# Layer 1 FFN up products: GpSimd's sums behind the gating, VectorE's block sums ahead of it and two blocks later

## The chip, the cores and the metric

The kernel runs on one core of one Trainium2 chip. The metric is the device time of one execution in microseconds; a kernel's time is the median over several executions. The engines are named as the profile names them: PE (TensorE matmul), PEld (its weight load), DVE (VectorE), ACT (ScalarE), POOL (GpSimd) and SP (the queue that issues the DMAs).

## What is computed

A two-layer trunk over 1024 latent and 256 context tokens, width 1024. Layer 0 mixes tokens by pooling, layer 1 by attention. Each layer ends with a gated FFN with a three-tap convolution over positions:

```
u = h @ w_up                       # (1024, 1024) @ (1024, 5632)
u = up[:-2]*conv_w[0] + up[1:-1]*conv_w[1] + up[2:]*conv_w[2] + conv_b
a, v = split(u, 2);  y = (silu(a) * v) @ w_down      # (1024, 2816) @ (2816, 1024)
```

The change lies in layer 1's `h @ w_up` and in what is prepared beside it for `@ w_down`.

## The kernel before

**Three matmuls for one.** Every float32 operand is split into a high part (a rounding copy on ACT, line 160) and a low part (source minus high part, line 161, mostly on POOL, some on DVE). `mm3` (lines 164 to 166) multiplies high by high, high by low and low by high.

**Blocks.** The 2816 gate columns and the 2816 value columns are cut into 22 blocks of 128. Block j works on gate columns and value columns j together, over 1024 tokens. Two columns of blocks and two halves of the inner dimension form a 2x2 by 2x2 block product, which is done with seven products instead of eight (Winograd's form of Strassen's scheme). In block j >= 3 PE runs products 1, 6, 2, 5, 7, 3, 4 in that order; each is 4 times `mm3`, 12 matmuls of 128x512. Products 6 and 5 share PSUM bank 6, products 7 and 4 share bank 4, products 1 and 2 share bank 0 or 2, by the block's parity. Block 0 is a plain product and blocks 1 and 2 mix in with it; they have their own order of products (`order`).

**What surrounds the products.** For block j the seven products need sums of the weights (`w_sums`, four on POOL, line 1492, from the raw weights `wraw` to the buffers `sf`) and six splits (`w_split`: 5 is the raw gate block, 1024 columns wide, 1, 0, 2, 3 are the sums, 4 the lower half of the raw value block; 512 wide). After the products come, from `up_acts`:

- a copy of product 1's bank by ACT (`s1c`, line 1567), which product 2 has to wait for;
- five DVE additions that read or write PSUM (`plus`, line 1528): `vsum` after product 6 (product 5 waits for it), `rsum` after 5, b3 after 7 (product 4 waits for it, since it adds to the bank that b3 reads), b1 after 3, b2 after 4;
- for either half: `ident` on ACT (line 1539, PSUM to SBUF with scale and bias), then two taps on DVE (line 1547); Silu on ACT for the gate half (line 1554);
- `gating` on DVE (line 1556, 128x1024, both inputs in SBUF), and the store of its result to `g_d[j]` in DRAM.

**Sums for the down projection.** The product with `w_down` is also done in seven products, of 11 blocks each, and needs sums of weights (`weights_sums`, stored to `tw_d`) and of gated units (`units_sums`, stored to `sg_d`): four 128x512 DVE operations per set (line 1673), both inputs in SBUF. From block 3 on, each block carries one set: sets of weights 0 to 7 in blocks 3 to 10, sets of units 0 to 10 in blocks 11 to 21; three sets of weights are done at the start of the down products. The buffers are `sum_a` and `sum_b`; loads and stores go through SP.

**The order on each engine.** A function that is due at time t in `acts` is issued as soon as the planned matmuls before it add up to t (`play`); a `mm3` of 512 columns is planned at 0.648 us, a product at 2.592, a block at 18.144. `end[j, p]` is the planned end of product p of block j. So due times set the order of instructions on each engine, and each engine runs its own in that order. For block j of the steady part, counted from the planned start of the block, DVE has before the change: vsum at 5.18, gating of block j-1 at 5.28, that block's four sums for the down projection at 6.63 to 9.93, rsum at 10.37, b3 at 12.96, b1 at 15.60, two taps, b2 at 18.45, two taps. POOL has the four `w_sums` of block j+1 from 0.30 on and its six low parts from 4.40 to 7.40.

Of the kernel before, what the change touches and what calls it, by code (L numbers as in the profile page):

```python
# [10 lines left out]
F32 = mybir.dt.float32  # L11
# [71 lines left out]
def backbone(ctx: ExitStack, tc: tile.TileContext, io, out: bass.AP):  # L83
# [1367 lines left out]
    sf_early, sf_late = ([at(o, HK, P) for o in q] for q in ((172, 174, 144, 146), (128, 130, 108, 110)))  # L1451
    gate_w = [hl(16, KT, P), hl(152, KT, P)]

    gate_early = [tuple(at(o, KT, P, r=True) for o in q) for q in ((108, 128), (136, 168))]
# [16 lines left out]
            nc.sync.dma_start(wraw[j, part], w_up1[:, :, c : c + P])  # L1471

    def sf_of(j):
        return sf_early if j == 1 else sf_late

    gate_third = at(136, KT, P, r=True), at(104, KT, P, r=True)
    sum_third = [hl(o, HK, P) for o in (96, 100, 16, 20, 196)]
# [19 lines left out]
    def w_split(j, which):
# [32 lines left out]
    def up_acts(j, end):  # L1530

        b = banks_of(j)
        b0, b1, bx, b2, b3 = (bank(n) for n in (b[1], b[3], 6, 4, 5))
        cv = conv[1]

        def ident(half):
            f = half * NJ + j
            src = psum[:, b[1] * 512 : (b[1] + 2) * 512] if half == 0 else psum[:, 4 * 512 : 6 * 512]
            nc.scalar.activation(cs1[half], src, AF.Identity, scale=cv[:, 1, f : f + 1], bias=cv[:, 3, f : f + 1])  # L1539

        def tap(half, t):
# [47 lines left out]
    def t_lo(m, eng):  # L1589
        eng.tensor_tensor(out=tsp[m][1], in0=tfs[m], in1=tsp[m][0].bitcast(F32), op=ALU.subtract)  # L1590
# [48 lines left out]
    acts += [(18.5, lambda: t_lo(1, nc.vector)), (18.6, lambda: t_lo(0, nc.vector))]  # L1639
    acts += [(18.7, lambda: w_split(1, 3)), (18.8, lambda: w_split(1, 0)), (18.9, lambda: w_load(2)), (20, lambda: w_split(1, 4)), (20.1, lambda: w_split(2, 5))]  # L1640
    acts += [(19 + 0.1 * n, lambda m=m, q=q: t_hi(m, q)) for n, (m, q) in enumerate(((2, 0), (2, 1), (3, 0), (3, 1)))]
    acts += [(end[0, "gate"] + 3, lambda: t_lo(2, nc.vector)), (end[0, "value"] + 3, lambda: t_lo(3, nc.vector))]
    for j in range(NJ):
        acts += up_acts(j, end)
    for j in range(2, NJ):
        t = end[j - 2, 4]
        for q in range(4):
            acts.append((t + (5.05 + 0.6 * (q - 2) if j == 2 and q > 1 else 0.3 + 0.01 * q), lambda j=j, q=q: w_sums(j)[q]()))
        for q, which in enumerate((5, 1, 0, 2, 3, 4)):
            if j > 2 or q:  # L1650
                acts.append((t + 4.4 + 0.6 * q, lambda j=j, which=which: w_split(j, which)))
        if j + 1 < NJ:
            acts.append((t + 0.1, lambda j=j: w_load(j + 1)))

# [17 lines left out]
    def tt2(o, x, y, op):  # L1672
        return lambda: nc.vector.tensor_tensor(out=o, in0=x, in1=y, op=op)  # L1673
# [4 lines left out]
    def units_sums(f):

        a11, a21 = sum_a[:, 0], sum_a[:, 1]  # L1680
        a12, a22 = cs1[1][:, 0:HC], cs1[1][:, HC:LAT]
        s1, s4 = sum_b[:, 0], sum_b[:, 1]

        def keep_sums():
            nc.sync.dma_start(sg_d[f][0], sum_a.rearrange("p a b -> p (a b)"))
            nc.sync.dma_start(sg_d[f][1], sum_b.rearrange("p a b -> p (a b)"))

        return [tt2(s1, a21, a22, ALU.add), tt2(a21, a11, a21, ALU.subtract), tt2(a11, s1, a11, ALU.subtract),
                tt2(s4, a12, a11, ALU.subtract), keep_sums]
# [12 lines left out]

    def sums_acts(j):

        t21 = max(end[j, 4] + 0.05, max(end[j, 3], end[j, 5] + 0.75) + 2.9)
        t = max(t21 + 4.1, end.get((j + 1, 6), 0) + 0.1)
        if j < NH2:
            f = j - 3
            r = [(end[j, 4] + 0.2, lambda: sums_load(w_dn[f], sum_a)), (end[j, 4] + 0.21, lambda: sums_load(w_dn[f + NH2], sum_b))]
            fns = weights_sums(f, sum_a, sum_b)  # L1710
        else:
            f = j - NH2
            r = [(end[j, 4] + 0.2, lambda: sums_load(g_d[f], sum_a))]
            fns = units_sums(f)
        return r + [(t + 1.35 + 1.1 * n, fn) for n, fn in enumerate(fns)]
# [140 lines left out]
```

## Time and profile before

| | us |
|---|---|
| median of 3 runs (lowest, highest) | 2270.13 (2269.89, 2270.99) |
| the profiled execution, its own time | 2274.05 |
| span of the profiled execution, first to last instruction | 2272.3 |
| PE busy in it | 2176.8 (96%) |
| DVE, POOL, ACT busy | 1466.7, 1368.6, 982.8 |

The profile is one execution. Busy shares are averages over stages that have different limits; matmuls are pipelined, so the start-to-start distance of matmuls tells more of PE's pace than their busy time.

### The profile page before, as it was taken

The numbers are of one execution on the slowest core, as the hardware profiler recorded it, in microseconds if no ns is written. First come the engines' busy times: TensorE is split into PE (matmuls) and PEld (weight loads), VectorE is DVE, ScalarE is ACT, GpSimd is POOL, SyncE is SP. The second block draws the span as 40 slices with busy tenths as digits, with TensorE's granted clock in tenths as the row PEclk, the third lists the DMA queues.
The fourth block names the chain that finished last, engine by engine and source line by source line (L and its number), as shares of the span: only waits on it lengthen the run. The fifth ranks groups of instructions, "written<-read, shape, count | busy, mean of one in ns | idle before, by whom it ended". The sixth has DMA issues, their size and how long they took to land.

```text
span 2272.3 us, 29713 instructions
## 1 busy us (share of the span) xinstructions
PE 2176.8 (96%) x11008; PEld 1794.8 (79%) x11008; DVE 1466.7 (65%) x1986; ACT 982.8 (43%) x1519; POOL 1368.6 (60%) x846
## 2 busy tenths in 40 slices
PE   7989999999999999999999999999999999999999
PEld 5768888888888878877877887777777777778887
DVE  5665545544556484457776666655768888888565
ACT  4364333433434233444446666644433333334442
POOL 0344666666665556753346777634677787764655
PEclk8999999999999999999999999999999999999999
DMA  8831221122127667740000122132235544448775
GB/s 312 290 124 58 68 83 61 61 82 70 61 77 245 214 239 237 242 154 19 32 21 24 62 65 75 47 102 78 81 102 177 194 162 144 158 157 327 258 241 184
DMA packets 191891, 306.06 MB, mean 135 GB/s; under 512 B 12658, under 2 KB 120066, under 8 KB 191746
## 3 DMA queue, kind: packets, MB, share of 16 engines
q1 hardware_dynamic: 191746, 304.17, 40.1%
q8 instruction: 86, 1.41, 0.3%
q14 instruction: 59, 0.48, 0.1%
HBM read 237.26 MB, written 66.86 MB: 134 GB/s over the span
## 4 chain that ended last, share of the span: by engine, by line
PE 59%; DVE 23%; ACT 6%; issue 6%; DMA 3%; POOL 2%; SPq 0%; ACTq 0%; DVEq 0%; POOLq 0%
PE psum L164 18%; PE psum L166 18%; PE psum L165 18%; DVE a L1673 5%; PE psum L1292 2%; DVE a L1547 2%; DVE a L1556 2%; ACT a L1539 2%; DVE a_512r L161 1%; DVE psum L1528 1%; DVE a L1274 1%; DVE a L1127 1%; POOL a_1024r L161 1%; DVE a L1035 1%; ACT a_512r L160 1%
## 5 line engine op out<-in xcount | busy, mean ns | idle before, releaser
L161 POOL TENSOR_TENSOR a_512r<-a,a_512r 128x512 fp32r<-128x512 f32 x366 | 539.3, 1491 | 297.0 <-ACT a_512r L160 265.9
L160 ACT CAST a_512r<-a 128x512 fp32r<-128x512 f32 (+1 forms) x509 | 291.6, 610 | 476.9 <-POOL a L621 188.0
L161 POOL TENSOR_TENSOR a_1024r<-a,a_1024r 128x1024 fp32r<-128x1024 f32 x106 | 273.3, 2581 | 260.3 <-ACT a_1024r L160 247.3
L164 PE MATMUL psum<-a_2048r,a_512r 128*128 128x512 f32 (+1 forms) x1008 | 358.7, 356 | 25.2 <-DVE psum L1528 20.3
L166 PE MATMUL psum<-a_2048r,a_512r 128*128 128x512 f32 (+1 forms) x1008 | 355.2, 353 | 0.0
L165 PE MATMUL psum<-a_4096r,a_512r 128*128 128x512 f32 x708 | 278.1, 393 | 0.0
L683 DVE SCALAR_TENSOR_TENSOR a<-psum,conv,a 128x255 f32<-128x255 f32 (+1 forms) x176 | 150.8, 879 | 147.6 <-ACT a L678 146.0
L164 PEld LDWEIGHTS psum<-a_2048r,a_512r 128*128 128x128 f32 x1008 | 191.4, 190 | 61.3 <-DVE psum L1528 27.4
L165 PE MATMUL psum<-a_2048r,a_512r 128*128 128x256 f32 (+1 forms) x688 | 231.2, 336 | 0.0
L161 DVE TENSOR_TENSOR a_512r<-a,a_512r 128x512 fp32r<-128x512 f32 (+1 forms) x143 | 141.8, 997 | 134.1 <-ACT a_512r L160 129.5
L166 PEld LDWEIGHTS psum<-a_2048r,a_512r 128*128 128x128 f32 x1008 | 191.0, 189 | 26.3
L164 PE MATMUL psum<-a_1024r,a_512r 128*128 128x512 f32 x440 | 172.5, 392 | 1.9 <-ACT a L1093 1.1
L166 PE MATMUL psum<-a_1024r,a_512r 128*128 128x512 f32 x440 | 171.4, 390 | 1.0 <-DVE a_512r L161 1.0
L165 PE MATMUL psum<-a_1024r,a_512r 128*128 128x512 f32 x440 | 171.3, 389 | 0.0
L1539 ACT ACTIVATE a<-psum,conv 128x1024 f32<-128x1024 f32 x44 | 53.1, 1206 | 264.5 <-DVE psum L1528 264.5
L164 PE MATMUL psum<-a_4096r,a_1024r 128*128 128x512 f32 x408 | 161.5, 396 | 2.7 <-ACT a L1567 2.7
L166 PE MATMUL psum<-a_4096r,a_1024r 128*128 128x512 f32 x408 | 159.9, 392 | 1.8 <-POOL a_1024r L161 1.8
L165 PE MATMUL psum<-a_4096r,a_1024r 128*128 128x512 f32 x408 | 159.4, 391 | 0.0
L164 PE MATMUL psum<-a_4096r,a_512r 128*128 128x512 f32 x388 | 152.9, 394 | 1.8 <-ACT a L716 1.8
L165 PEld LDWEIGHTS psum<-a_4096r,a_512r 128*128 128x128 f32 x708 | 133.8, 189 | 25.7 <-POOL a_4096r L767 0.4
L166 PE MATMUL psum<-a_4096r,a_512r 128*128 128x512 f32 x388 | 152.4, 393 | 0.0
L1547 DVE SCALAR_TENSOR_TENSOR a<-psum,conv,a 128x1023 f32<-128x1023 f32 x88 | 112.9, 1282 | 60.2 <-ACT a L1539 58.7
(241 smaller groups left out, 5001.2 us busy)
## 6 DMA issues: line engine op xcount, KB each, us to landing
a<-in_ada_w_dram SPq DMA_DIRECT2D x96, 512.0 KB
a<-in_ffn_w_up_dram SPq DMA_DIRECT2D x88, 512.0 KB
a<-in_ffn_w_down_dram SPq DMA_DIRECT2D x88, 512.0 KB
g_d<-a SPq DMA_DIRECT2D x44, 512.0 KB
x_d<-a SPq DMA_DIRECT2D x26, 512.0 KB
tw_d<-a SPq DMA_DIRECT2D x22, 512.0 KB
sg_d<-a SPq DMA_DIRECT2D x22, 512.0 KB
a<-tw_d SPq DMA_DIRECT2D x44, 256.0 KB
```

Of the source, the lines that this page charges most:

```text
L160: nc.scalar.copy(hi, src)
L161: (lo_eng or nc.gpsimd).tensor_tensor(out=lo, in0=src, in1=hi.bitcast(F32), op=ALU.subtract)
L164: nc.tensor.matmul(ps, lh, rh, start=first, stop=False, skip_group_check=shared)
L165: nc.tensor.matmul(ps, lh, rl, start=False, stop=False, skip_group_check=shared)
L166: nc.tensor.matmul(ps, ll, rh, start=False, stop=last, skip_group_check=shared)
L683: nc.vector.scalar_tensor_tensor(out=dst[:, lo:hi], in0=src[:, lo + d : hi + d], scalar=cv[:, t, f : f + 1], in1=dst[:, lo:hi], op0=ALU.mu ...
L1035: nc.vector.tensor_scalar(out=o, in0=pt[:, q * P : (q + 1) * P], scalar1=sc, scalar2=sh, op0=ALU.mult, op1=ALU.add)
L1292: nc.tensor.transpose(pt[:, h * P : (h + 1) * P], probs[(4 * u + h) % len(probs)][:, k * P : (k + 1) * P], ident)
L1539: nc.scalar.activation(cs1[half], src, AF.Identity, scale=cv[:, 1, f : f + 1], bias=cv[:, 3, f : f + 1])
L1547: nc.vector.scalar_tensor_tensor(out=c[:, lo:hi], in0=psum[:, o + lo + d : o + hi + d], scalar=cv[:, t, f : f + 1], in1=c[:, lo:hi], op0=A ...
L1556: (tg, lambda: nc.vector.tensor_tensor(out=cs1[1], in0=cs1[0], in1=cs1[1], op=ALU.mult)),
L1673: return lambda: nc.vector.tensor_tensor(out=o, in0=x, in1=y, op=op)
```

## The change

For blocks 4 to 21 the weight sums on POOL are due only after the gating of the block before (planned 0.3 us after product 6's end, 0.2 after the gating's due time), and their first buffer is moved to offset 188, where the gating's first input (`cs1[0]`) lies, so they also have to wait for it. The low parts are spread over the block: the raw gate block's split and the raw value block's split around the block's start, splits 0 and 1 between the sums, splits 2 and 3 after product 1 of the next block. The Silu is due after product 1 of the next block. On DVE the four sums for the down projection are due right behind vsum, ahead of the gating, and block j's own set is done in block j instead of behind the gating of block j in block j+1: sets of weights 0 to 9 in blocks 3 to 12, sets of units 0 to 8 in blocks 13 to 21 (two blocks later than before); weights 10 and units 9 and 10 are done at the start of the down products. The units' sums are made from two loads instead of one load and the gating's result in SBUF; the loads are due in product 7 of the block before. The halves of the second stored sum change places, so products 3 and 5 of the down projection read each other's half. Product 1 of block 2 comes ahead of product 7 of block 1, product 6 of block 2 ahead of its product 2, and the convolution of block 0 and two low parts (`t_lo(2)`, `t_lo(3)`) are due at other times.

```diff
-    sf_early, sf_late = ([...] for q in ((172, 174, 144, 146), (128, 130, 108, 110)))
+    sf_early, sf_late, sf_gate = ([at(o, HK, P) for o in q] for q in ((172, 174, 144, 146), (128, 130, 108, 110), (188, 130, 108, 110)))
...
-        return sf_early if j == 1 else sf_late
+        return sf_early if j == 1 else sf_late if j < 4 else sf_gate
...
-                (t12 + 3.8, lambda: nc.scalar.activation(cs1[0], cs1[0], AF.Silu)),
+                (max(t12 + 3.8, end.get((j + 1, 1), 0) + 0.15 if j else 0), lambda: nc.scalar.activation(cs1[0], cs1[0], AF.Silu)),
...
-            t12, t21 = end[0, "gate"] - 0.75, end[0, "value"] + 0.95
-            return conv_of(t12, t21, t21 + 4.1)
-        t12 = max(end[j, 3], end[j, 5] + 0.75) + 0.05
+            fns, t = [fn for _, fn in conv_of(0, 0, 0)], end[0, "value"]
+            times = end[0, "gate"] + 0.05, t - 4.5, t - 3.5, t + 0.3, t + 0.05, end[1, 6] + 0.02, end[1, 6] + 0.03, end[1, 6] + 0.3, end[1, 6] + 1.6
+            return list(zip(times, fns))
+        t12 = max(end[j, 3], end[j, 5] + 0.75, end[j, 7]) + 0.05
...
-    order = [(1, 6), (1, 3), (1, 5), (1, 7), (2, 1), (1, 4)] + [(2, p) for p in (2, 6, 5, 7, 3, 4)]
+    order = [(1, 6), (1, 3), (1, 5), (2, 1), (1, 7), (1, 4)] + [(2, p) for p in (6, 2, 5, 7, 3, 4)]
...
-    acts += [(end[0, "gate"] + 3, lambda: t_lo(2, nc.vector)), (end[0, "value"] + 3, lambda: t_lo(3, nc.vector))]
+    acts += [(end[1, 6] + 0.1, lambda: t_lo(2, nc.vector)), (end[1, 6] + 0.2, lambda: t_lo(3, nc.vector))]
...
+        else:
+            hi, lo = ([lambda j=j, w=w, h=h: split_parts(j, w)[h]() for w in range(6)] for h in range(2))
+            sums = [lambda j=j, q=q: w_sums(j)[q]() for q in range(4)]
+            tg, tn = end[j - 1, 6] + 0.3, end[j, 1]
+            acts += [(t - 1.4, hi[5]), (t - 0.5, lo[5]), (t + 0.06, hi[4]), (t + 0.07, lo[4]),
+                     (tg, sums[0]), (tg + 1.3, hi[0]), (tg + 1.31, sums[1]), (tg + 2.6, hi[1]), (tg + 2.61, lo[0]),
+                     (tg + 3.9, lo[1]), (tg + 5.2, sums[2]), (tg + 6.5, sums[3]),
+                     (tn + 0.05, hi[2]), (tn + 0.06, hi[3]), (tn + 0.07, lo[2]), (tn + 0.08, lo[3])]
...
+    side_sums = [(w_dn, weights_sums, f) for f in range(NH2 - 1)] + [(g_d, units_sums, f) for f in range(NH2)]
+    side_sums.append((w_dn, weights_sums, NH2 - 1))
     for j in range(3, NJ):
-        acts += sums_acts(j)
+        src, make, f = side_sums[j - 3]
+        fns, stores = make(f, sum_a, sum_b)
+        t = end[j, 6] + 0.02
+        acts += [(end[j - 1, 7] + 0.1 + 0.01 * q, lambda src=src, f=f, q=q, w=w: sums_load(src[f + q * NH2], w))
+                 for q, w in enumerate((sum_a, sum_b))]
+        acts += [(t + 0.01 * m, fn) for m, fn in enumerate(fns)] + [(t + 3 + 0.1 * q, fn) for q, fn in enumerate(stores)]
...
+    for n, m in enumerate((2, 0, 1)):
+        src, make, f = side_sums[NJ - 3 + m]
...
+        t = (base - 4.5, base - 4.4, base + 10)[n]
...
+        t = base + (8.2, 13.8, 20.2)[n]
+        acts += [(t + 1.36 * q, fn) for q, fn in enumerate(fns)] + [(t + 5.5 + 0.1 * q, fn) for q, fn in enumerate(stores)]
```

## Rows read from the trace of the kernel before

**Rows 1.** Waits from 1690 to 2040 us: which instruction's line waited for which, us in total, times, longest.
```profile
PEld psum L164 <- DVE psum L1528: 27.4, 17, 2.0
PE psum L164 <- DVE psum L1528: 20.3, 17, 1.5
```

**Rows 2.** Timeline of PE: the first matmuls of blocks 3, 4 and 21 and of the down products, and around the wait ahead of product 4 in blocks 4 and 20 (the first and the last of 17). Columns: start, duration, engine, line, operation, tiles, shapes, idle before and who ended it.
```profile
1669.38 0.39 PE L164 MATMUL psum<-a_4096r,a_1024r 128*128 128x512 f32 x1
...
1688.63 0.39 PE L164 MATMUL psum<-a_4096r,a_1024r 128*128 128x512 f32 x1
...
1706.78 0.50 PE L164 MATMUL psum<-a_2048r,a_512r 128*128 128x512 f32 x1 [1.54 <-DVE psum L1528]
...
2033.47 0.39 PE L166 MATMUL psum<-a_4096r,a_512r 128*128 128x512 f32 x1
2035.03 0.50 PE L164 MATMUL psum<-a_2048r,a_512r 128*128 128x512 f32 x1 [1.18 <-DVE psum L1528]
...
2037.88 0.39 PE L164 MATMUL psum<-a_4096r,a_1024r 128*128 128x512 f32 x1
...
2056.92 0.39 PE L164 MATMUL psum<-a_512r 128*128 128x512 f32 x1
```

**Rows 3.** Timeline of DVE over one block of the steady part, the same columns.
```profile
1777.22 0.68 DVE L1528 TENSOR_TENSOR a<-psum,a 128x512 f32<-128x512 f32 x1
1777.82 2.79 DVE L1556 TENSOR_TENSOR a<-a,a 128x1024 f32<-128x1024 f32 x1
1780.53 1.77 DVE L1673 TENSOR_TENSOR a<-a 128x512 f32<-128x512 f32 x1
1782.34 3.36 DVE L1673 TENSOR_TENSOR a<-a,a 128x512 f32<-128x512 f32 x2
...
1787.33 0.68 DVE L1528 TENSOR_TENSOR a<-psum,a 128x512 f32<-128x512 f32 x1
1788.11 1.30 DVE L1528 TENSOR_TENSOR psum<-psum,a 128x512 f32<-128x512 f32 x2
1790.74 2.60 DVE L1547 SCALAR_TENSOR_TENSOR a<-psum,conv,a 128x1023 f32<-128x1023 f32 x2 [1.33 <-ACT a L1539]
1793.26 0.69 DVE L1528 TENSOR_TENSOR psum<-psum,a 128x512 f32<-128x512 f32 x1
1795.22 2.60 DVE L1547 SCALAR_TENSOR_TENSOR a<-psum,conv,a 128x1023 f32<-128x1023 f32 x2 [1.27 <-ACT a L1539]
```

**Rows 4.** Timeline of POOL over the same stretch.
```profile
1777.12 2.41 POOL L161 TENSOR_TENSOR a_1024r<-a,a_1024r 128x1024 fp32r<-128x1024 f32 x1 [3.97 <-ACT a_1024r L160]
1779.49 9.04 POOL L161 TENSOR_TENSOR a_512r<-a,a_512r 128x512 fp32r<-128x512 f32 x5
...
1789.84 3.79 POOL L1492 TENSOR_TENSOR a<-a,a 128x512 f32<-128x512 f32 x3
```

**Rows 5.** Block 3, which carries no sums for the down projection, and block 21, where POOL has almost nothing to do: DVE's timeline (b1 of block 3, two sums of block 21) and POOL's (one row each).
```profile
1686.12 0.70 DVE L1528 TENSOR_TENSOR psum<-psum,a 128x512 f32<-128x512 f32 x1 [2.02 <-PE psum L166]
...
2048.01 0.69 DVE L1673 TENSOR_TENSOR a<-a 128x512 f32<-128x512 f32 x1
2048.74 0.69 DVE L1673 TENSOR_TENSOR a<-a,a 128x512 f32<-128x512 f32 x1
...
1678.20 7.25 POOL L161 TENSOR_TENSOR a_512r<-a,a_512r 128x512 fp32r<-128x512 f32 x5
2043.89 3.53 POOL L161 TENSOR_TENSOR a_512r<-a,a_512r 128x512 fp32r<-128x512 f32 x2 [9.20 <-ACT a_512r L160]
```

**Rows 6.** The chain of work that ended last, within 1777 to 1800 us, in order of time: start, us, what.
```profile
1787.43 3.35 DMA tw_d<-a
1790.79 7.44 DMA a<-in_ffn_w_down_dram
```

**Rows 7.** Timeline of PE between blocks 1 and 3: the last matmul ahead of the first of four gaps, the matmuls behind the other three, and one of those that follow the third.
```profile
1632.11 0.39 PE L166 MATMUL psum<-a_4096r,a_512r 128*128 128x512 f32 x1
...
1639.09 0.47 PE L164 MATMUL psum<-a_2048r,a_512r 128*128 128x512 f32 x1 [2.41 <-DVE a L1547]
1650.19 0.50 PE L164 MATMUL psum<-a_4096r,a_1024r 128*128 128x512 f32 x1 [2.67 <-ACT a L1567]
1652.22 0.63 PE L165 MATMUL psum<-a_4096r,a_1024r 128*128 128x512 f32 x1
1658.36 0.50 PE L164 MATMUL psum<-a_2048r,a_512r 128*128 128x512 f32 x1 [0.79 <-DVE a L1528]
```

**Rows 8.** The same stretch on DVE, POOL and ACT: the taps of block 0 and `t_lo(2)`, the first weight sum of block 2, and the copy `s1c` of block 2.
```profile
1628.11 2.60 DVE L1547 SCALAR_TENSOR_TENSOR a<-psum,conv,a 128x1023 f32<-128x1023 f32 x2 [2.09 <-ACT a L1539]
1630.63 2.32 DVE L1590 TENSOR_TENSOR a_2048r<-a,a_2048r 128x2048 fp32r<-128x2048 f32 x1
...
1631.19 2.89 POOL L1492 TENSOR_TENSOR a<-a 128x512 f32<-128x512 f32 x1 [0.40 <-DMA a<-in_ffn_w_up_dram]
1649.57 0.57 ACT L1567 COPY a<-psum 128x512 f32<-128x512 f32 x1
```

**Rows 9.** Granted clock (the column behind the engines' busy times), DMA share and GB/s over two stretches, and PE's one wait over half a microsecond in the down products.
```profile
1690.00:2040.00 350.00, 329.73 (x1433) 267.31 (x1432) 300.55 (x240) 125.48 (x170) 275.31 (x167) 1.00 0.49 161
1630.00:1660.00 30.00, 22.94 (x91) 17.55 (x90) 20.71 (x17) 13.62 (x18) 28.71 (x19) 0.94 0.42 124
...
2090.67 0.50 PE L166 MATMUL psum<-a_512r 128*128 128x512 f32 x1 [0.50 <-DVE a_512r L161]
```

More of the change, by code (lines that the diff above doesn't have):

```diff
@@ L1450, in backbone @@
     raws = Ring(at(o, D) for o in (168, 172, 208, 212))
-    sf_early, sf_late = ([at(o, HK, P) for o in q] for q in ((172, 174, 144, 146), (128, 130, 108, 110)))
+    sf_early, sf_late, sf_gate = ([at(o, HK, P) for o in q] for q in ((172, 174, 144, 146), (128, 130, 108, 110), (188, 130, 108, 110)))
     gate_w = [hl(16, KT, P), hl(152, KT, P)]
@@ L1495, in w_sums, with split_parts @@
                 op(3, a12, sf[1], ALU.subtract)]
+    def split_parts(j, which):
+        (hi, lo), src = (gate_of(j), wraw[j, 0]) if which == 5 else (
+            sums_of(j)[which], sf_of(j)[which] if which < 4 else wraw[j, 1][:, HK:])
+        return (lambda: nc.scalar.copy(hi, src),
+                lambda: nc.gpsimd.tensor_tensor(out=lo, in0=src, in1=hi.bitcast(F32), op=ALU.subtract))
     def w_split(j, which):
@@ L1646, in backbone @@
         t = end[j - 2, 4]
[L1647 to L1653, printed above, removed]
+        acts += [(t + 0.1, lambda j=j: w_load(j + 1))] if j + 1 < NJ else []
+        if j < 4:
+            for q in range(4):
+                acts.append((t + (5.05 + 0.6 * (q - 2) if j == 2 and q > 1 else 0.3 + 0.01 * q), lambda j=j, q=q: w_sums(j)[q]()))
+            for q, which in enumerate((5, 1, 0, 2, 3, 4)):
+                if j > 2 or q:
+                    acts.append((t + 4.4 + 0.6 * q, lambda j=j, which=which: w_split(j, which)))
+        else:
[6 more added lines that the diff above has]
+                     (tn + 0.05, hi[2]), (tn + 0.06, hi[3]), (tn + 0.07, lo[2]), (tn + 0.08, lo[3])]
     NH2, HC = NJ // 2, 512
@@ L1665, in backbone @@
     G_AT = {1: lambda f: g_d[f][:, 0:HC], 2: lambda f: g_d[f + NH2][:, 0:HC], 4: lambda f: g_d[f + NH2][:, HC:LAT],
-            5: lambda f: sg_d[f][1][:, 0:HC], 3: lambda f: sg_d[f][1][:, HC:LAT],
+            3: lambda f: sg_d[f][1][:, 0:HC], 5: lambda f: sg_d[f][1][:, HC:LAT],
             6: lambda f: sg_d[f][0][:, 0:HC], 7: lambda f: sg_d[f][0][:, HC:LAT]}
@@ L1676, in sums_load, with kept @@
         nc.sync.dma_start(dst.rearrange("p a b -> p (a b)"), src)
[L1678 to L1689, printed above, removed]
+    def kept(dst, wa, wb):
+        return [lambda q=q, w=w: nc.sync.dma_start(dst[q], w.rearrange("p a b -> p (a b)")) for q, w in enumerate((wa, wb))]
@@ L1691, in weights_sums, with units_sums @@
+    def units_sums(f, wa, wb):
+        a11, a21, a12, a22 = wa[:, 0], wa[:, 1], wb[:, 0], wb[:, 1]
+        return [tt2(a22, a21, a22, ALU.add), tt2(a21, a11, a21, ALU.subtract), tt2(a11, a22, a11, ALU.subtract),
+                tt2(a12, a12, a11, ALU.subtract)], kept(sg_d[f], wa, wb)
     def weights_sums(f, wa, wb):
         b11, b12, b21, b22 = wa[:, 0], wa[:, 1], wb[:, 0], wb[:, 1]
-        def keep_sums():
-            nc.sync.dma_start(tw_d[f][0], wa.rearrange("p a b -> p (a b)"))
-            nc.sync.dma_start(tw_d[f][1], wb.rearrange("p a b -> p (a b)"))
@@ L1698, in weights_sums @@
         return [tt2(b11, b12, b11, ALU.subtract), tt2(b12, b22, b12, ALU.subtract), tt2(b22, b22, b11, ALU.subtract),
-                tt2(b21, b21, b22, ALU.subtract), keep_sums]
+                tt2(b21, b21, b22, ALU.subtract)], kept(tw_d[f], wa, wb)
     base = span(pe)
[L1703 to L1715, printed above, removed]
@@ L1717, in backbone @@
-    for j in range(3, NJ):
-        acts += sums_acts(j)
-    for n, f in enumerate(range(NH2 - 3, NH2)):
-        wab = [at(o, 2, HC) for o in ((64, 68), (72, 76), (80, 84))[n]]
-        t = (base - 4.5, base - 4.4, base + 0.5)[n]
-        acts += [(t + 0.01 * q, lambda f=f, q=q, w=wab[q]: sums_load(w_dn[f + q * NH2], w)) for q in range(2)]
-        acts += [(base + 13.2 + 1.36 * (4 * n + m), fn) for m, fn in enumerate(weights_sums(f, *wab))]
+    side_sums = [(w_dn, weights_sums, f) for f in range(NH2 - 1)] + [(g_d, units_sums, f) for f in range(NH2)]
@@ new lines, in backbone @@
+    side_sums.append((w_dn, weights_sums, NH2 - 1))
+    for j in range(3, NJ):
+        src, make, f = side_sums[j - 3]
[6 more added lines that the diff above has]
+        src, make, f = side_sums[NJ - 3 + m]
+        wab = [at(o, 2, HC) for o in ((64, 68), (72, 76), (80, 84))[n]]
+        t = (base - 4.5, base - 4.4, base + 10)[n]
+        acts += [(t + 0.01 * q, lambda src=src, f=f, q=q, w=wab[q]: sums_load(src[f + q * NH2], w)) for q in range(2)]
+        fns, stores = make(f, *wab)
+        t = base + (8.2, 13.8, 20.2)[n]
+        acts += [(t + 1.36 * q, fn) for q, fn in enumerate(fns)] + [(t + 5.5 + 0.1 * q, fn) for q, fn in enumerate(stores)]
```

## The prediction

> **What bounds the kernel now.** I read the waits of the stage first. Between 1690 and 2040 us PE waits for one kind of instruction only, an addition of `plus` on DVE, once in each of 17 blocks [rows 1]. PE's timeline shows where: ahead of product 4, which adds to the bank that b3 still has to read. The wait is 1.54 us in block 4 and 1.18 in block 20, where the next matmul starts 1.56 us after the last one instead of 0.23 [rows 2]. Next the block's length. Block 21 has no such wait and takes 2056.92 - 2037.88 = 19.04 us for 84 matmuls; so a product is 2.72 us. Blocks 4 to 20 take (2037.88 - 1688.63) / 17 = 20.54 us, 1.50 more each. Block 3 takes 19.25 [rows 2].
>
> Then DVE's timeline, to see why b3 is late. Gating and the four sums for the down projection stand between vsum and rsum and take from 1777.82 to 1787.4 us, 9.6 us [rows 3]. A sum of 512 elements takes 1.67 to 1.77 us there. In block 21, after POOL's last instruction there, the same operation takes 0.69 [rows 5]. POOL's timeline gives the cause: its low parts run from 1777.12 to 1788.5, five of them at 9.04 / 5 = 1.81 us each; the weight sums that meet only additions and taps, which take one operand from PSUM, need 3.79 / 3 = 1.26 [rows 4]. The taps keep 2.60 the pair meanwhile [rows 3]. So operations with two SBUF inputs on DVE and POOL take turns: 0.6 + 1.26 is the 1.8 of either. Block 3 separates the two: POOL works there, the four sums are absent, and PE has no wait of that kind.
>
> A rule agrees and says who gives way. The Trainium skill, "SBUF — State Buffer", section "Who interferes with whom", states that DVE with two SBUF inputs and a reading GpSimd instruction use one interface, held for a whole instruction by whichever started first. By the rule and by the rows a collision costs the same; what hangs on the rule is only the first rival's mechanism.
>
> **The change, block by block.** I walk one block from 4 on, u = us after its first matmul; products end at 2.72, 5.44, 8.16, 10.88, 13.60, 16.32, 19.04.
>
> DVE: b1 starts 0.2 after product 3 (block 3: 1686.12, against 1688.63 - 2.72 = 1685.91 [rows 2, 5]), at u = 16.5. From b1's start (1788.76) to the end of the last tap (1797.82) DVE and ACT need 9.06 [rows 3], so the taps end at 25.6, 6.55 of the next block. vsum follows until 7.2. Now come the four sums, while POOL should be idle: 4 x 0.7 = 2.8 [rows 5], until 10.0. The gating is never seen alone; from below it is two 512-wide operations at 0.6, 1.2; from above it is today's 2.79 [rows 3]. I take 1.2, since POOL waits for it: 11.2. With 0.5 for a meeting with POOL's last low part (below) it ends at 11.7. rsum ends at 12.4, b3 (product 7 + 0.2 + 0.7) at 14.5, and product 4 starts at 16.32 without waiting: 1.8 to spare.
>
> POOL: sum 0 starts at 11.7. Two sums and low part 0 at 1.27 (low parts lie between 1.26 and block 3's 7.25 / 5 = 1.45, where the gating still interrupts one [rows 4, 5]) end at 15.5; low part 1 and sums 2, 3 at 19.4; the 1024-wide low part (2.41 [rows 4]) at 21.8; low part 4 at 23.1, 4.1 of the next block. Low parts 2 and 3 need ACT: ident starts 1.27 ahead of its taps [rows 3], at 2.7, takes 1.2, then the copy for product 2 (0.57 [rows 8]) ends at 4.5, ahead of that product's start at 5.44, and two casts of 0.6 follow. So these parts run from 5.1 to 7.7 and meet the first DVE sum, which is due at 7.2: the 0.5 above. POOL works 14 us of 19.04. Every operand is ready: product 6 of the next block has low part 1 by 16.8, product 7 has low part 2 by 6.4 against 10.88.
>
> New waits: sum 0 lies in the gating's input buffer. Behind it on POOL wait all the other sums and the splits; ident of the block (u = 17.2) overwrites that buffer and has to wait for low part 0, done at 15.5: 1.7 to spare. The closed loop from gating to gating is 3.8 (POOL) + 8.4 (ident to last tap) + 0.65 + 2.8 + 0.5 + 1.2 = 17.35 us, below 19.04. The Silu moves behind the copy and two casts and is done by 6.8; the gating needs it at 10.
>
> SP: stores of the sums go out at 10.0 and, behind the gating's store, at 11.7; they land 3.35 later and the next loads take 7.44 [rows 6]: 3.5 of the next block, 3.7 ahead of their use. Nine blocks load 0.5 MB more; the engines were 0.49 busy [rows 9], so I cost this at nothing, with those 3.7 us as its cover.
>
> So blocks 3 to 21 should all take 19.04: today 2056.92 - 1669.38 = 387.54, then 19 x 19.04 = 361.76: **25.8 us less**. If each keeps block 3's 0.21 [rows 2], 4 less is gained.
>
> **The first blocks.** From 1632.11 to 1669.38 PE does 120 matmuls (27.4 us with the step into them) in 37.27: 9.9 lost in four gaps and in a stretch at half the matmul rate (0.43 a step from 1652.22 on, which is 1.2 of 2.4 GHz) [rows 7]; the granted clock averages 0.94 there [rows 9]. Walked anew: DVE does the taps until 1630.7 [rows 8], then vsum, block 0's other taps, until 1634.0; product 5 of block 1 (1632.34) and product 1 of block 2 run without a gap. `t_lo(2)` and `t_lo(3)`, 2.2 each, alternate with a low part of POOL and end at 1639.7; sum 2 on POOL and the gating end at 1642.0, then rsum and b3 end at 1643.4. Product 4 of block 1 could start at 1640.5: **a gap of 2.9**. If DVE wins the turns it is 0.9, if POOL gets one more, 4.2. Then ACT's copy for block 2 ends at 1646.3, its ident at 1647.5, two taps, b2, ident and one tap at 1653.4 and vsum at 1654.1; product 5 of block 2 could start at 1651.7: **2.4 more**. After that nothing waits; with 0.2 for slow first matmuls 5.5 is lost instead of 9.9, 4.4 gained. The slow stretch costs about 2 today (9 matmuls at 0.2). It followed two gaps of 2.4 and 2.7 us of idling in 14 us; the new gaps are as large and as near, so I charge half, 1.0: **3.4 gained**, bounds 1.5 and 6.
>
> **Down products.** After block 21 DVE had 16 sums (units 10, weights 8 to 10), now 12, as dense as before; PE waits there 0.5 us once [rows 9]. Units 9 and 10 load what DVE and SP have stored shortly before. I take 0, from 0.5 better to 3 worse.
>
> **Sum.** 25.8 + 3.4 = 29.2. The profiled execution took 2274.05 (span 2272.3), so 2244.9; the median stands 3.9 below it, so 2270.1 - 29.2 = **2241**.
>
> **The rivals.** First, slower: the collisions stay. POOL's low parts 2 and 3 hang on ACT, and if POOL runs late its queue meets the four sums and the gating again. Then the loop is 3.8 + 8.4 + 0.65 + 6.8 + 2.8 = 22.4 us, 1.9 above 20.54, for 18 blocks 34 us: 2270 - 3 + 34 = 2301. It turns slower when the loop passes 20.54, from three collisions of 1.07 (1.67 - 0.6) beyond the one counted. Against it: sum 0 cannot start before the gating, so at most those two low parts can be there. Second, half the gain: product 5 waits for vsum, which is ready at 7.2 against 8.16, only 1.0 to spare, and two more casts now stand between a block's two idents (1.9 to spare). A slip of 0.7 beyond the cover costs 13 over 19 blocks: 2254. Third, nothing: a load or a store lands 3.7 us later than today's rows say and holds DVE's queue, rsum and b3 behind it; about 2268.
>
> **How the numbers follow.** Forecast 0.74, half the gain 0.13, nothing 0.04, slower 0.09. The forecast's own range is 2234 to 2248 (first blocks, block 3's 0.21, down products); up to 2256 takes in most of the half gain. About 0.2% is what a measurement tells from no change, here 4.5 us: faster 0.87, same 0.04, slower 0.09.
>
> **What would show it.** Right: DVE's sums at 0.6 to 0.7 us, no PE wait ahead of product 4, blocks of 19.04, POOL's sum 0 starting at the end of the gating. Wrong: sums still at 1.7, PE waits ahead of product 5 or 7, an ident that waits for POOL, or DVE that waits for a DMA.

## The result and the profile after

The changed kernel takes 2239.28 us (median of 4 runs, 2234.95 to 2244.01) where the kernel before took 2270.01 beside it on the same chip (4 runs, 2265.29 to 2270.99): the ratio is 0.9869, 95% interval 0.9845 to 0.9894. The forecast was 2241, its range 2234 to 2256. The profiled execution took 2238.29 us, with a span of 2236.5.

The page after, span and busy time:

```profile
span 2236.5 us, 29672 instructions
PE 2162.4 (97%) x11008; PEld 1791.3 (80%) x11008; DVE 1380.7 (62%) x1986; ACT 987.0 (44%) x1519; POOL 1322.0 (59%) x846
```

DVE is busy for 86 us less and POOL for 47, though each does nearly the same operations: time in which one engine held the other up was counted as busy (a sum of 512 columns took 1.7 us beside POOL and 0.69 without it [rows 3, 5]).

PE's timeline after: the two waits that are left between blocks 1 and 3, the first matmul of block 3, the one wait within the blocks (block 21) and the first matmul of the down products.

```profile
1638.08 0.50 PE L164 MATMUL psum<-a_2048r,a_512r 128*128 128x512 f32 x1 [2.38 <-DVE psum L1534]
1648.21 0.50 PE L164 MATMUL psum<-a_2048r,a_512r 128*128 128x512 f32 x1 [1.64 <-DVE a L1534]
1659.22 0.39 PE L164 MATMUL psum<-a_4096r,a_1024r 128*128 128x512 f32 x1
...
2016.10 0.47 PE L164 MATMUL psum<-a_4096r,a_512r 128*128 128x512 f32 x1 [0.40 <-DVE a_512r L161]
2021.66 0.39 PE L164 MATMUL psum<-a_512r 128*128 128x512 f32 x1
```

Blocks 3 to 21 take 2021.66 - 1659.22 = 362.44 us, against 387.54 [rows 2]. The waits from 1690 to 2020 us (who waited for whom, us in total, times, longest) have no line in which PE waits for an addition of DVE:

```profile
POOL a L1492 <- DVE a L1562: 67.0, 17, 3.9
DVE psum L1534 <- PE psum L166: 65.0, 35, 2.0
PE psum L164 <- DVE a_512r L161: 0.4, 1, 0.4
```

The wait of [rows 1] has turned round. There PE waited 20.3 us in 17 blocks; the 27.4 us of its weight loads are the same 17 waits seen on its other queue, so the two do not add up. DVE now waits for PE, and POOL waits for the gating (line 1562 now) once a block, as its new operand asks. DVE's timeline in the block that begins at 1792.50, and POOL's (`plus` is now line 1534, the sums for the down projection 1691, the taps 1553, the low parts 1501):

```profile
1799.02 0.68 DVE L1534 TENSOR_TENSOR a<-psum,a 128x512 f32<-128x512 f32 x1
1799.61 1.02 DVE L1691 TENSOR_TENSOR a<-a 128x512 f32<-128x512 f32 x1
1800.67 1.42 DVE L1691 TENSOR_TENSOR a<-a,a 128x512 f32<-128x512 f32 x2
1802.12 0.69 DVE L1691 TENSOR_TENSOR a<-a 128x512 f32<-128x512 f32 x1
1802.73 1.22 DVE L1562 TENSOR_TENSOR a<-a,a 128x1024 f32<-128x1024 f32 x1
1803.87 0.68 DVE L1534 TENSOR_TENSOR a<-psum,a 128x512 f32<-128x512 f32 x1
1806.30 0.70 DVE L1534 TENSOR_TENSOR psum<-psum,a 128x512 f32<-128x512 f32 x1 [1.75 <-PE psum L166]
1809.02 0.70 DVE L1534 TENSOR_TENSOR psum<-psum,a 128x512 f32<-128x512 f32 x1 [2.02 <-PE psum L166]
1811.05 2.60 DVE L1553 SCALAR_TENSOR_TENSOR a<-psum,conv,a 128x1023 f32<-128x1023 f32 x2 [1.33 <-ACT a L1545]
```

```profile
1793.00 2.42 POOL L1501 TENSOR_TENSOR a_1024r<-a,a_1024r 128x1024 fp32r<-128x1024 f32 x1 [0.33 <-ACT a_1024r L1500]
1797.53 2.56 POOL L1501 TENSOR_TENSOR a_512r<-a,a_512r 128x512 fp32r<-128x512 f32 x2 [0.87 <-ACT a_512r L1500]
1804.03 1.29 POOL L1492 TENSOR_TENSOR a<-a 128x512 f32<-128x512 f32 x1 [3.94 <-DVE a L1562]
...
1809.14 2.55 POOL L1492 TENSOR_TENSOR a<-a,a 128x512 f32<-128x512 f32 x2
```

From the first sum to rsum DVE needs 1803.87 - 1799.61 = 4.26 us, where the same five operations took 9.51 [rows 3]. Only the first sum is held up (1.02 for 0.7), by the end of the low parts that start at 1797.53. b3, the operation that PE had waited for, now waits 1.75 us for PE.

The granted clock (the column behind the five engines' busy times) over the blocks and over the first gaps:

```profile
1690.00:2020.00 330.00, 329.60 (x1454) 272.60 (x1454) 217.22 (x243) 129.66 (x173) 234.38 (x170) 1.00 0.57 194
1630.00:1650.00 20.00, 15.99 (x70) 12.55 (x69) 15.31 (x13) 8.44 (x13) 19.60 (x12) 1.00 0.24 79
```

Where the time went, from PE's and DVE's timelines of all profiled runs. "To tap" ends at the first tap of block 0 and holds no changed code; "head" goes from there to the first matmul of block 3; "blocks" to the first down product; "rest" to the end. Stretch is DVE's time from the end of vsum to rsum in one block. The last column is the median over that of the kernel before, whose own medians lay between 2268.1 and 2270.0.

| kernel | to tap | head | blocks 3-21 | one block (mean of 4-20) | stretch | rest | span | ratio (95%) |
|---|---|---|---|---|---|---|---|---|
| before | 1628.11 | 41.27 | 387.54 | 20.54 | 9.5 | 215.38 | 2272.3 | |
| changed | 1623.17 | 36.05 | 362.44 | 19.04 | 4.3 | 214.84 | 2236.5 | 0.9869 (0.9845 to 0.9894) |
| pool_only | 1619.35 | 42.15 | 362.14 | 19.04 | 7.2 | 215.86 | 2239.5 | 0.9897 (0.9878 to 0.9917) |
| dve_only | 1622.81 | 41.31 | 389.02 | 20.52 | 9.5 | 214.16 | 2267.3 | 0.9997 (0.9988 to 1.0006) |
| early_only | 1628.91 | 36.08 | 387.84 | 20.57 | - | 215.07 | 2267.9 | 0.9988 (0.9975 to 1.0001) |
| narrow_sums | 1626.85 | 41.28 | 364.55 | 19.19 | 7.7 | 214.22 | 2246.9 | 0.9900 (0.9873 to 0.9928) |
| own_buffer | 1620.41 | 36.12 | 370.54 | 19.53 | 8.3 | 214.83 | 2241.9 | 0.9900 (0.9882 to 0.9918) |
| new_head | 1622.7 | 34.8 | 362.4 | 19.04 | - | 214.8 | 2234.7 | 0.9861 (0.9844 to 0.9877) |
| new_head2 | 1625.91 | 31.57 | 362.88 | 19.04 | - | 214.74 | 2235.1 | 0.9853 (0.9839 to 0.9866) |

Before to changed the spans differ by 35.8: 25.10 in the blocks, 5.22 in the head, 0.54 in the rest and 4.94 ahead of the first tap, where the program is the same. Without those 4.94 it is 30.9, and the medians differ by 30.7.

### The profile page after: what moved, and what is told of

Same layout as the page of the kernel before. It is cut to its first block, busy times and chain, and to the rows that moved or that the text cites. A ratio compares the mean times of both kernels' runs of the same rounds, so it can differ in the third digit from the quotient of the medians.

```text
span 2236.5 us, 29672 instructions
## 1 busy us (share of the span) xinstructions
PE 2162.4 (97%) x11008; PEld 1791.3 (80%) x11008; DVE 1380.7 (62%) x1986; ACT 987.0 (44%) x1519; POOL 1322.0 (59%) x846
## 4 chain that ended last, share of the span: by engine, by line
PE 75%; DVE 12%; ACT 5%; issue 5%; POOL 2%; DMA 2%; SPq 0%; ACTq 0%; DVEq 0%; POOLq 0%
PE psum L164 23%; PE psum L166 23%; PE psum L165 23%; PE psum L1292 3%; DVE a L1274 1%; POOL a_1024r L161 1%; DVE a_512r L161 1%; DVE a L1127 1%; ACT a_512r L160 1%; PE psum L313 1%; DVE a L1035 1%; PE psum L394 1%; POOL a_4096r L161 1%; DVE hs L1094 1%; ACT a L1017 0%
## 5 line engine op out<-in xcount | busy, mean ns | idle before, releaser
L161 POOL TENSOR_TENSOR a_512r<-a,a_512r 128x512 fp32r<-128x512 f32 x276 | 376.9, 1380 | 285.7 <-ACT a_512r L160 254.5
L160 ACT CAST a_512r<-a 128x512 fp32r<-128x512 f32 (+1 forms) x419 | 243.0, 607 | 478.2 <-POOL a L621 189.1
L161 POOL TENSOR_TENSOR a_1024r<-a,a_1024r 128x1024 fp32r<-128x1024 f32 x88 | 229.7, 2614 | 184.2 <-ACT a_1024r L160 169.4
L164 PEld LDWEIGHTS psum<-a_2048r,a_512r 128*128 128x128 f32 x1008 | 191.4, 190 | 35.2 <-DVE psum L1534 2.8
L166 PEld LDWEIGHTS psum<-a_2048r,a_512r 128*128 128x128 f32 x1008 | 191.3, 190 | 25.9
L165 PEld LDWEIGHTS psum<-a_2048r,a_512r 128*128 128x128 f32 x688 | 131.2, 191 | 15.4
```

Of the source, the lines that this page charges most:

```text
L160: nc.scalar.copy(hi, src)
L161: (lo_eng or nc.gpsimd).tensor_tensor(out=lo, in0=src, in1=hi.bitcast(F32), op=ALU.subtract)
L164: nc.tensor.matmul(ps, lh, rh, start=first, stop=False, skip_group_check=shared)
L165: nc.tensor.matmul(ps, lh, rl, start=False, stop=False, skip_group_check=shared)
L166: nc.tensor.matmul(ps, ll, rh, start=False, stop=last, skip_group_check=shared)
```

## The experiments

**The changed kernel again.** The same program was run twice more beside experiments.

> The changed kernel once more, beside the other two on the same chip: blocks 3 to 21 at 19.04 to 19.1 us, head 36 to 38 us by whether the clock falls there, total 2235 to 2244; what differs from the first run should lie in the opening 130 us and in the head, not in the blocks.

> The changed kernel beside the other head on the same chip: head 36.05 us, blocks 3 to 21 in 362.4 us, as in both runs so far; total 2235 to 2241.

Measured: 2237.56 (2234.92 to 2239.57) and 2239.48 (2238.95 to 2240.03), ratios 0.9866 and 0.9868. Head, blocks and rest repeat within 0.1, 0.1 and 0.7 us (36.05 and 36.07; 362.45 and 362.43; 215.54 and 214.88), while the first tap starts at 1619.06 and 1623.82. So what two traces say of the head or the blocks can be compared to a tenth, of the rest to 0.7, their spans only to some 5 us, and most of that difference lies in the opening.

**POOL's part alone: pool_only.** The kernel before with the new queue of POOL, its buffer and the later Silu; the four sums on DVE stay behind the gating.

```diff
-        return sf_early if j == 1 else sf_late
+        return sf_early if j == 1 else sf_late if j < 4 else sf_gate
...
+            acts += [(t - 1.4, hi[5]), (t - 0.5, lo[5]), (t + 0.06, hi[4]), (t + 0.07, lo[4]),
+                     (tg, sums[0]), (tg + 1.3, hi[0]), (tg + 1.31, sums[1]), (tg + 2.6, hi[1]), (tg + 2.61, lo[0]),
```

> Only the change on POOL and ACT (weight sums behind the gating, in its buffer, the splits spread out, the later Silu); DVE's sums for the down projection stay behind the gating. Theory of turns between DVE and POOL: the gating now runs free of POOL at 1.2 us, but then the four DVE sums and POOL's sums start together and alternate, about 1.7 us each, so rsum and b3 still come late: PE waits 0.3 to 1.1 us ahead of product 4, blocks of 19.4 to 20.1 us instead of 20.54, about 2257 in all. Rival, that the place of POOL's work alone was the fault: blocks of 19.04, about 2245.

Measured: 2245.37 us, ratio 0.9897; blocks of 19.04, all of the blocks' gain. The expected wait of 0.3 to 1.1 us a block (about 2257 in all) did not come; the block and the time are those of the rival. DVE's timeline in one block:

```profile
1782.88 1.56 DVE L1562 TENSOR_TENSOR a<-a,a 128x1024 f32<-128x1024 f32 x1
1784.36 0.68 DVE L1687 TENSOR_TENSOR a<-a 128x512 f32<-128x512 f32 x1
1785.08 3.36 DVE L1687 TENSOR_TENSOR a<-a,a 128x512 f32<-128x512 f32 x2
1788.47 1.67 DVE L1687 TENSOR_TENSOR a<-a 128x512 f32<-128x512 f32 x1
1790.06 0.68 DVE L1534 TENSOR_TENSOR a<-psum,a 128x512 f32<-128x512 f32 x1
1790.84 0.70 DVE L1534 TENSOR_TENSOR psum<-psum,a 128x512 f32<-128x512 f32 x1
1792.29 0.70 DVE L1534 TENSOR_TENSOR psum<-psum,a 128x512 f32<-128x512 f32 x1 [0.74 <-PE psum L166]
```

Three sums still take 1.67 to 1.7, since POOL's sums run beside them (the first from 1784.52, 1.67 us against 1.29 in the changed kernel). But the gating takes 1.56 instead of 2.79 and the first sum 0.68 instead of 1.77 [rows 3], so rsum begins 7.2 us after the gating did and not 9.5. b3 follows rsum without waiting and product 4 is not late. The kernel before missed its time by 1.5 us a block; 2.3 were enough. What the DVE part adds is cover: in the changed kernel b3 waits 1.75 us for PE. The rest of pool_only's distance from the changed kernel is its old head: 42.15 - 36.05 = 6.1 of the 6.4 us between the two ratios (0.9897 - 0.9869, of 2270). That this head is 0.9 longer than in the kernel before was not looked into.

**The DVE part alone: dve_only.** The sums before the gating and two blocks later, with their loads and stores; POOL's queue as before.

```diff
+        t = end[j, 6] + 0.02
+        acts += [(end[j - 1, 7] + 0.1 + 0.01 * q, lambda src=src, f=f, q=q, w=w: sums_load(src[f + q * NH2], w))
+                 for q, w in enumerate((sum_a, sum_b))]
+        acts += [(t + 0.01 * m, fn) for m, fn in enumerate(fns)] + [(t + 3 + 0.1 * q, fn) for q, fn in enumerate(stores)]
```

> Only the change on DVE (sums for the down projection ahead of the gating, loads a product 7 earlier, units two blocks later, three sets at the start of the down products); POOL as before. Theory of turns: POOL's low parts meet the same five DVE operations, only in another order, so gating and sums still take about 9.6 us, blocks stay at 20.4 to 20.6, total 2268 to 2271. Rival, that the round of store, load and sums set the pace (1787.43 + 3.35, then 7.44, then gating and four sums, which is nearly a block of 20.5): the earlier loads break it and blocks fall to 19.04, about 2245.

Measured: 2268.39, ratio 0.9997 (0.9988 to 1.0006), blocks of 20.52. DVE's five operations between vsum and rsum with rsum itself, and the largest wait of PE's weight loads from 1700 to 2015 us:

```profile
1773.87 2.26 DVE L1673 TENSOR_TENSOR a<-a 128x512 f32<-128x512 f32 x1
1776.16 3.36 DVE L1673 TENSOR_TENSOR a<-a,a 128x512 f32<-128x512 f32 x2
1779.56 1.66 DVE L1673 TENSOR_TENSOR a<-a 128x512 f32<-128x512 f32 x1
1781.14 2.31 DVE L1556 TENSOR_TENSOR a<-a,a 128x1024 f32<-128x1024 f32 x1
1783.38 0.68 DVE L1528 TENSOR_TENSOR a<-psum,a 128x512 f32<-128x512 f32 x1
...
PEld psum L164 <- DVE psum L1528: 25.6, 16, 1.6
```

The order on DVE moves the 9.5 us about and shortens them by nothing, since POOL's five low parts (9.04 us here as before [rows 4]) meet whichever five operations stand there. The rival that the loop of store, load and sums had been the bound falls with it: here that loop is new and the time is old.

**The first blocks alone: early_only.** The new order of products, the times of block 0's convolution and of the two low parts.

```diff
-    order = [(1, 6), (1, 3), (1, 5), (1, 7), (2, 1), (1, 4)] + [(2, p) for p in (2, 6, 5, 7, 3, 4)]
+    order = [(1, 6), (1, 3), (1, 5), (2, 1), (1, 7), (1, 4)] + [(2, p) for p in (6, 2, 5, 7, 3, 4)]
...
-    acts += [(end[0, "gate"] + 3, lambda: t_lo(2, nc.vector)), (end[0, "value"] + 3, lambda: t_lo(3, nc.vector))]
+    acts += [(end[1, 6] + 0.1, lambda: t_lo(2, nc.vector)), (end[1, 6] + 0.2, lambda: t_lo(3, nc.vector))]
```

> Only the change to the first blocks (order of products of blocks 1 and 2, block 0's convolution, the two low parts). From block 0's first tap to block 3's first matmul 36 to 37 us as in the changed kernel, against 41.27 before; blocks 4 to 20 stay at 20.54; total 4 to 5 below before, about 2265. If the early gain hung on the rest of the change, nothing is gained here.

Measured: 2266.51, 1.6 us below the kernel before where 4 to 5 were expected, ratio 0.9988 (0.9975 to 1.0001), so the runs alone leave open whether it gained. The trace does not: the head takes 36.08 instead of 41.27. Which of its parts (the order of products, the convolution, the low parts) brings this was not run apart. Its two gaps on PE, and the windows over them here and in own_buffer (below):

```profile
1643.85 0.79 PE L164 MATMUL psum<-a_2048r,a_512r 128*128 128x512 f32 x1 [2.40 <-DVE psum L1528]
1653.96 0.50 PE L164 MATMUL psum<-a_2048r,a_512r 128*128 128x512 f32 x1 [0.16 <-DVE a L1528]
...
1636.00:1656.00 20.00, 17.43 (x70) 13.60 (x69) 15.33 (x13) 8.57 (x13) 19.59 (x12) 0.91 0.24 79
```

```profile
1628.00:1648.00 20.00, 17.53 (x69) 13.67 (x69) 15.32 (x13) 9.02 (x13) 19.58 (x13) 0.91 0.24 79
```

Here the granted clock did fall between the two gaps (0.91 on average over the 20 us), as it had before the change [rows 7, 9], and it cost nothing: the slower matmuls used up the second wait, 0.16 instead of 1.64, and block 3 starts 36.08 us after the first tap instead of 36.05 at full clock. DVE and ACT set this stretch, not PE.

**Is it the operands or the length of the sums? narrow_sums.** The kernel before, with the four sums for the down projection made on 32 of 512 columns.

```diff
-        a11, a21 = sum_a[:, 0], sum_a[:, 1]
-        a12, a22 = cs1[1][:, 0:HC], cs1[1][:, HC:LAT]
+        a11, a21 = sum_a[:, 0, :32], sum_a[:, 1, :32]
+        a12, a22 = cs1[1][:, 0:32], cs1[1][:, HC:HC + 32]
```

> The kernel before, with each of the four DVE sums for the down projection done on 32 of its 512 columns (the other columns of these sums are left out). Theory of turns, an operation waits until the other engine's whole instruction is done: a sum still takes about 1.3 us in blocks 4 to 20, its wait for one POOL instruction, and gating plus sums 8 us instead of 9.6. Rival, that the two engines share a rate: a sum of 32 columns takes 0.1 to 0.2 us, gating plus sums 3.4. In both PE's wait ahead of product 4 should go, since 1.5 us is enough.

Measured: 2245.85 (2 runs), ratio 0.9900. DVE's timeline in one block, one sum of block 21 after POOL's last low part there, POOL's low parts beside the first rows and, last, the only wait of PE's queues from 1700 to 2015 us:

```profile
1790.39 2.79 DVE L1556 TENSOR_TENSOR a<-a,a 128x1024 f32<-128x1024 f32 x1
1793.10 1.27 DVE L1673 TENSOR_TENSOR a<-a 128x32 f32<-128x32 f32 x1
1794.41 2.46 DVE L1673 TENSOR_TENSOR a<-a,a 128x32 f32<-128x32 f32 x2
1796.90 1.21 DVE L1673 TENSOR_TENSOR a<-a 128x32 f32<-128x32 f32 x1
1798.04 0.68 DVE L1528 TENSOR_TENSOR a<-psum,a 128x512 f32<-128x512 f32 x1
...
2023.61 0.19 DVE L1673 TENSOR_TENSOR a<-a 128x32 f32<-128x32 f32 x1
...
1792.05 7.27 POOL L161 TENSOR_TENSOR a_512r<-a,a_512r 128x512 fp32r<-128x512 f32 x5
...
PEld psum L164 <- ACT a L1567: 3.9, 16, 0.3
```

A sum of 32 columns takes 1.21 to 1.27 us, nearly twice what 512 columns take when POOL is quiet (0.69 [rows 5]). It has almost nothing to do itself: in block 21, with POOL quiet, the same 32 columns take 0.19. Beside POOL its time is that of one low part of POOL (1.27), and the rival, a shared rate with 0.1 to 0.2 us a sum, falls. This is the waiting for a turn seen by itself. The Trainium skill, "SBUF — State Buffer", section "SBUF: two separate sides", has it so: of a DVE instruction with two SBUF inputs and a GpSimd instruction that reads SBUF, whichever starts first holds the shared pair for the whole instruction, and the other blocks; these rows agree, with 1.21 to 1.27 us for a sum of 0.19.

PE has no wait ahead of product 4 here. The 0.15 us by which these blocks exceed 19.04 lie at the start of product 2, whose weight loads wait for ACT's copy of product 1's bank (the last row).

**Is the wait on the gating needed? own_buffer.** The changed kernel with the first weight sum in its old buffer, so that POOL may start it before the gating is done.

```diff
-        return sf_early if j == 1 else sf_late if j < 4 else sf_gate
+        return sf_early if j == 1 else sf_late
```

> The changed kernel with one thing undone: the weight sums of blocks 4 to 21 go to the old buffer (offset 128) and not to the gating's input, so that POOL's first sum need not wait for the gating; all due times are the changed kernel's. Theory of turns: POOL starts its sums while DVE is at the four sums, all five DVE operations meet a POOL instruction, gating ends near 16.4 us of the block, b3 near 17.7, PE waits 1.0 to 1.5 us ahead of product 4, blocks of 20.0 to 20.6, total 2258 to 2267. Rival, that the due times alone keep the two apart: blocks of 19.04, 2236 to 2242.

Measured: 2245.37 where the changed kernel took 2237.56 on the same chip; blocks of 19.53, 370.54 in all. DVE in one block, and the wait of PE's weight loads from 1700 to 2015 us:

```profile
1779.91 1.02 DVE L1691 TENSOR_TENSOR a<-a 128x512 f32<-128x512 f32 x1
1780.96 3.37 DVE L1691 TENSOR_TENSOR a<-a,a 128x512 f32<-128x512 f32 x2
1784.36 1.67 DVE L1691 TENSOR_TENSOR a<-a 128x512 f32<-128x512 f32 x1
1785.95 2.31 DVE L1562 TENSOR_TENSOR a<-a,a 128x1024 f32<-128x1024 f32 x1
...
PEld psum L164 <- DVE psum L1534: 9.6, 16, 1.7
```

POOL's first sum starts at 1780.34, right behind its low parts, and takes 1.74 us; from there on everything meets: the stretch is 8.3 us, and PE's weight loads wait again, 0.6 us a block. The direction was as expected, the size was not: a block is 0.49 longer than 19.04, where 1.0 to 1.5 were expected. So the shared buffer is worth 370.54 - 362.44 = 8.1 us, by nothing but the order that it forces.

**The two gaps that are left: new_head and new_head2.** Product 6 of block 2 goes ahead of product 4 of block 1, block 0's gating and block 1's convolution later, and block 2's later splits 7.7 us later.

```diff
-    order = [(1, 6), (1, 3), (1, 5), (2, 1), (1, 7), (1, 4)] + [(2, p) for p in (6, 2, 5, 7, 3, 4)]
+    order = [(1, 6), (1, 3), (1, 5), (2, 1), (1, 7), (2, 6), (1, 4)] + [(2, p) for p in (2, 5, 7, 3, 4)]
```

> The changed kernel with another order at the head: product 6 of block 2 ahead of product 4 of block 1, block 0's gating behind b3 of block 1, b2 of block 1 between its first two taps, three splits of block 2 behind block 1's ident. Theory that each of the two gaps left there is one late DVE addition (b3, then vsum): both close, from block 0's first tap to block 3's first matmul 36.05 us becomes 31.2 to 32.5, total 4 below the changed kernel. Rival, that a wait moves on to the next product that reads DVE's results (product 7 of block 2 behind its taps): 33 to 36.

Measured: 2236.95, head 34.8 instead of 36.05. In this kernel block 2's vsum is written before b2 of block 1 has read block 1's, so that one addition has another operand than it should. Both old gaps went and a new one came, behind the first matmul of product 3 of block 2:

```profile
1652.16 0.50 PE L165 MATMUL psum<-a_4096r,a_512r 128*128 128x512 f32 x1 [3.10 <-POOL a_1024r L161]
```

The profile ends this wait with the low part of block 3's gate weights (2.34 us on POOL, from 1649.76), which had slipped behind three splits and the four sums of block 3 on POOL. Product 3 does not read that part itself, so what it waits for was not settled. new_head2 moves three of those sums behind it, and block 2's vsum behind b2 of block 1:

```diff
-            (end[j, 6], lambda: plus(vsum, bx, s1c[j % 2])),
+            (end[j, 6] if j != 2 else end[1, 4] + 0.055, lambda: plus(vsum, bx, s1c[j % 2])),
...
-                acts.append((t + (5.05 + 0.6 * (q - 2) if j == 2 and q > 1 else 0.3 + 0.01 * q), lambda j=j, q=q: w_sums(j)[q]()))
+                acts.append((t + (5.05 + 0.6 * (q - 2) if j == 2 and q > 1 else 4.41 + 0.01 * q if j == 3 and q else 0.3 + 0.01 * q), lambda j=j, q=q: w_sums(j)[q]()))
```

> The changed kernel with another head: product 6 of block 2 ahead of product 4 of block 1, block 0's gating behind b3 of block 1, b2 of block 1 between its first two taps and vsum of block 2 behind it, three splits of block 2 behind block 1's ident, three sums of block 3 behind its widest split. Each of the two gaps of the changed kernel's head (2.77 and 2.03 us) is one late DVE addition: both close, from block 0's first tap to block 3's first matmul 36.05 us becomes 31.2 to 32.5, total 3.5 to 5 below the changed kernel. Rival, that the wait only moves on to a later product of block 2: 33 to 36, total as the changed kernel's.

Measured: head 31.57, 4.5 less than the changed kernel, and the new gap is gone. The first matmul of block 3 on PE, 31.57 us after the first tap at 1625.91:

```profile
1657.48 0.39 PE L164 MATMUL psum<-a_4096r,a_1024r 128*128 128x512 f32 x1
```

The time is 2235.95 (2234.23 to 2238.36) against 2239.48 of the changed kernel on the same chip: 3.5 us, 0.16%, in the direction of the trace, though no more than the runs spread.

## Why the prediction was right

**What bounds it.** Right, and shown. The waits of [rows 1] are gone, the five DVE operations fell from 9.51 to 4.26 us, and narrow_sums shows that most of their length had been POOL's and not their own. Undoing the separation (own_buffer) brings the wait back.

**The blocks, 25.8 forecast, 25.1 measured.** Blocks 4 to 20 take 19.04 on average. The 0.7 lies in block 21, nearly all of it in one new wait ahead of product 3 (0.40 by its row, 0.56 by the starts, since the matmul before starts at 2015.31 and the usual step is 0.23). The walk held nearly to the tenth (u from 1792.50): vsum ends at 7.2 (7.2), POOL's low parts 2 and 3 run from 5.0 to 7.6 (5.1 to 7.7), the gating ends at 11.45 (11.7), b1 starts at 16.5 (16.5), the raw gate block's low part ends at 2.9 of the next block (2.8). The gating alone takes 1.22, the lower of the two bounds. The collision charged 0.5 cost 0.35.

**What the walk did not see.** It gave the gain to both parts together. pool_only shows that POOL's part alone brings all of it and dve_only that the other alone brings nothing. The rows of before said so: the block was 1.5 us late, so that the stretch of 9.5 had to fall to about 8.0 and no further. The runs lie near that: a stretch of 9.5 loses 1.50 a block, one of 8.3 loses 0.49 (own_buffer), and at 7.7 (narrow_sums), 7.2 and 4.3 product 4 does not wait. By subtraction the limit is 7.8 to 8.0.

**The first blocks, 3.4 forecast, 5.2 measured.** Here one term was mis-sized. Without the charge for a slow stretch the walk gives 41.27 - 4.4 = 36.9 from the first tap to block 3, measured 36.05: its gaps of 2.9 and 2.4 came as 2.5 and 1.8 (2.77 and 2.03 from start to start, less the usual 0.23). That is 0.8 of the 1.8 by which the forecast fell short. The other 1.0 is the mis-sized term, the charge for half a slow stretch. The clock stayed at 1.00 in the changed kernel, but that is not the reason: in early_only and own_buffer it fell to 0.91 and the head was 36.08 and 36.12. The term stood on a stretch in which PE waits for DVE anyway, so the price of a slow PE was at most 0.07 us there.

**Down products, 0 forecast, 0.5 better measured.** Three profiles of the changed kernel differ by 0.7 in that stretch, so no difference is shown.

**The sum.** 29.2 forecast, 30.7 by the medians. The runs do not tell the two apart; the trace does, stretch by stretch. The blocks gave 0.7 less than forecast and the first blocks 1.8 more.

**The rivals.** The collisions that stay: the only one left is the first sum's 0.35, since POOL ran on time. The nearest to it that was run is own_buffer, where the collisions do stay: 8.1 us over 19 blocks, and still 1% faster than before. But there POOL does not wait for the gating, so the closed loop on which the rival's 34 us rested is not in it, and that price stays untested. Half the gain: neither vsum nor ident is late, since PE's only wait in the stretch is the 0.4 us of block 21, for a low part made on DVE. Nothing: DVE has no wait for a DMA in the blocks.

## What to carry to other kernels

When DVE and POOL take turns, find the time by which the consumer is late and free that much; what is freed beyond it is cover, and here 1.5 of 9.5 us was all that PE felt. Moving only one of the two queues can bring nothing (dve_only) or all (pool_only), so ask which of them decides what stands beside what. A wait through a shared buffer is a cheap way to hold two queues apart (8 us here), if the held queue has slack, and a slower PE is charged nothing in a stretch that another engine sets.

## What was not expected

- A 32-column sum takes 1.21 to 1.27 us beside POOL's low parts and 0.19 without them: the cost of a small operation on two SBUF inputs is here the other engine's instruction, not its own length. Taps with one operand in PSUM keep 2.60 the pair while POOL works, after as before [rows 3].
- The granted clock over the head differs between profiles with the same code there, 1.00 in the changed kernel and 0.91 in own_buffer, both after an idle PE of about 2.4 us. What decides it was not settled; it moved the head by less than 0.1 us.
- Executions of one program differ by up to 10 us (19 of the kernel before lie between 2263.6 and 2273.5), and the profiles put most of it into the opening. The weight loads of one line there, line 313 (first and last start behind the durations), end 6 us later in the profile of before, the first line, than in that after, the second:

```profile
L313 PEld LDWEIGHTS psum<-a,c_t x384: 106/109/155, 27.1 to 136.1; 128*32 128x32 f32 x192
```

```profile
L313 PEld LDWEIGHTS psum<-a,c_t x384: 106/109/153, 26.5 to 130.1; 128*32 128x32 f32 x192
```

Changes of a few us, such as early_only's or new_head2's, are seen in the stretch that they touch before they are seen in the total.
